# New step costs and a GpSimd wait in the timing model that orders the instructions of a two-layer diffusion block

## The chip, the core and the metric

The kernel runs on one core of a Trainium2 chip. A core has five engines that run side by side, each with its own queue of instructions in program order: TensorE (PE in the profile; PEld is its weight load), VectorE (DVE), ScalarE (ACT), GpSimd (POOL) and SyncE (SP). The time of a run is device microseconds from launch to end. Three timed runs of the kernel before gave 1829.44, 1833.56 and 1835.29 us, median 1833.56 us.

## The reference

Two layers over 512 latent tokens and 256 context tokens, width 1024, all in fp32:

```python
for i in range(DEPTH):                                   # DEPTH = 2
    sh1, sc1, g1, sh2, sc2, g2 = adaln(c, ada_w[i], ada_b[i])
    h_lat = modulate(rms_norm(x, norm_mix[i]), sh1, sc1)
    h_ctx = modulate(rms_norm(ctx, norm_mix[i]), csh1, csc1)
    if i % 2 == 0:   # 8 window-attention heads (a sink each) and 8 neighbourhood heads
        y_lat, y_ctx = even_mixer(h_lat, h_ctx, ...)
    else:            # latent attention: 16 heads, q and k of 64 + 32 columns
        y_lat, y_ctx = odd_mixer(h_lat, h_ctx, ...)
    x = x + g1 * y_lat
    x = x + g2 * squared_relu_mlp(modulate(rms_norm(x, norm_mlp[i]), sh2, sc2), mlp_w1[i], mlp_w2[i])
    # in layer 0 the context tokens get the same two updates
```

In both mixers heads are normalised (and partly rotated), scores are `q @ k` over the token's own selection and all 256 context keys in one softmax, and `p @ v` is projected with the output weights.

## The kernel before

Each fp32 operand of a product is split in a high and a low half (names with `h` and `l`: `wh_`, `wl_`, `hh_`, `hl_`), and a product is three TensorE matmuls. A split is a rounding copy (the high half, on ScalarE or VectorE) and a subtraction (the low half, on VectorE or GpSimd).

The kernel is straight-line code that runs through five stages: norms and conditioning; the even mixer (`mixer0`); the first MLP with the even output projection; the odd mixer (`mixer1`); the odd output projection and the second MLP. In a mixer nine or so streams of work are open at once: projections (`g_...` are their PSUM tiles), preparation of q and k (`qr_`, `ur_`, `ut_`, `qt_`, `kt_`, results in `q_`, `k_`, `kb`), scores of one head pair after another (`c_` the context part, `l_` the local part, reductions to `mx_` and `nm_`, exponentials into `P_`), values (`pp_` are transposes of P, `pt_` or `P` their copies, `o_` the products with v, `rs_`/`rb_` the division), and fillers of other stages (`ada_`, `ps_`). A digit in a name is the job and a last one the half: `c410` is the context score of the odd mixer's fifth pair, second half, first head. The window pairs are `a0` to `a3` with the context's own pairs `ac0` to `ac3`; the neighbourhood pairs are `b...`; the odd mixer's eight pairs are `c0` to `c7`.

What is written out next is decided while the kernel is built, by a model of the engines. Every instruction passes through `Engine`, which emits it and calls `Clock.note`: that adds a cost by engine and shape to the engine's time, after the operands are done and the destination is free (`LAG` is added between engines). All instructions therefore carry the line of that wrapper, L120. Three things read the model:

- `begins` and `weave` (lines 205 to 250): each stream stands at a `yield` with what it needs; the one that could start first on TensorE by the model goes on, and a tie goes to the earlier one in the list.
- `pick`, `pick2`, `square`, `scale_by` (lines 414 to 431, 943 to 952): which of two engines takes a copy, a low half, a square or a scaling is the one that the model has free first.
- `Weights.pump` (line 388): a weight that has landed is split when the model says that its raw data and its buffers are there.

The products of the MLPs and the output projections are in loops without `weave`; there the model moves single copies and splits only.

Of the kernel before, what the change touches and what calls it, by code (L numbers as in the profile page):

```python
# [10 lines left out]
F32 = mybir.dt.float32  # L11
# [16 lines left out]
class Clock:  # L28
# [5 lines left out]
    def __init__(self):  # L34
        self.t = defaultdict(float)
        self._done = defaultdict(lambda: (0.0, None))
        self._used = defaultdict(lambda: (0.0, None))

    @staticmethod
    def keys(a):  # L40
# [26 lines left out]
    def note(self, eng, fn, args, kw):  # L67
        aps = [a for a in list(args) + list(kw.values()) if hasattr(a, "tensor") and hasattr(a, "free_size")]
        outs = aps[:1] + [kw[k] for k in ("accum_out",) if k in kw]
        ins = aps[1:]  # L70
        n = max(a.free_size() for a in aps)
        psum = any(a.space == bass.MemoryType.PSUM for a in aps)
        if eng == "pe":
            if fn == "transpose":
                cost = 0.107
            else:
                f = 4 if aps[1].dtype == F32 else 1
                m = aps[0].partition_size()
                cost = max(aps[2].free_size() * f / 2400 * (0.5 if m <= 64 else 1.0),
                           0.107 * (2 if f == 4 and m > 64 else 1))  # L80
                if m <= 32:
                    cost = 0.109
        elif eng == "act":
            cost = (0.19 if psum else 0.094) + n / 1200 + (0.047 if "accum_out" in kw else 0)
        elif eng == "dve":
            two = len(ins) > 1 and ins[1].free_size() > 1
            cost = 0.07 + n / (960 if two or psum or fn.startswith("reduce") else 1920)
        elif eng == "pool":
            cost = 0.14 + n * 2.11 / 1000
        else:  # L90
            b = 1
            for s in outs[0].shape:
                b *= s
            self.t["dma"] = max([self.t["dma"], self.t["pe"]] + [self.used(a, "dma") for a in outs]) + b * 4 / 350e3
            for a in outs:
                self.set_done(a, self.t["dma"] + 2.0, "dma")
            return
        start = self.t[eng]
        for a in ins:
            start = max(start, self.done(a, eng))  # L100
        for a in outs:
            start = max(start, self.used(a, eng))
        end = start + cost
        self.t[eng] = end
        for a in ins:
            self.set_used(a, end, eng)
        for a in outs:
            self.set_done(a, end, eng)
            self.set_used(a, end, eng)
# [2121 lines left out]
```

## Time and profile before

| | |
|---|---|
| median of the runs | 1833.56 us |
| the profiled execution | 1835.26 us |
| its span | 1833.2 us |
| TensorE busy | 1744.4 us, 95% |
| VectorE busy | 1106.3 us, 60% |
| ScalarE busy | 668.1 us, 36% |
| GpSimd busy | 442.1 us, 24% |
| mean granted TensorE clock | 0.978 |

The profile is of one execution; its span is 2.06 us shorter than its time. TensorE's idle time, the span less 1744.4 us, is 88.8 us. Times in a row are microseconds from the start of the span; a group "x4" is four instructions of one kind in a row, and what stands in brackets behind it is the idle time of its engine just before, with the engine and the operation that ended it. Tile names in these rows have their numbers left out, so place and time tell which pair a row belongs to.

### The profile page before, as it was taken

The page shows a single profiled execution, that of the slowest core. Times are in us where ns is not written, and L with a number is a line of the kernel's source. Part 1 is how long each engine was busy: PE and PEld are TensorE (multiplying, and loading weights), DVE is VectorE, ACT ScalarE, POOL GpSimd, SP SyncE. Part 2 cuts the span into 40 slices and gives each one's busy share as a digit, 9 for nine tenths or more (in the row PEclk, how much of TensorE's full clock was granted, in tenths as well). Part 3 has the DMA queues.
Part 4 walks back from the last instruction along what each step waited for, and adds up shares of the span by engine and source line. Part 5 has one row for each costly group of instructions (what it writes and reads, how often), then busy time and mean ns, then how long its engine had stood idle before and what let it go on. Part 6 is the DMA issues. An engine that isn't in the chain of part 4 may idle for free.

```text
span 1833.2 us, 27762 instructions
## 1 busy us (share of the span) xinstructions
PE 1744.4 (95%) x11288; PEld 1469.0 (80%) x11288; DVE 1106.3 (60%) x1930; ACT 668.1 (36%) x1430; POOL 442.1 (24%) x288
## 2 busy tenths in 40 slices
PE   8889999888999999999999998899999999999999
PEld 6777777676878888888888897677665798989897
DVE  6877576755777666455454747778775652525252
ACT  4445444434233123123122234555554242424241
POOL 3212312122212222222221322302120223232322
PEclk9999999999989999999999999899999999999999
DMA  9234400010533334333431221001000223232332
GB/s 294 81 127 124 124 24 21 24 44 12 173 115 115 127 127 136 121 129 121 138 115 58 70 68 40 25 1 36 23 13 1 69 93 92 93 103 85 101 93 81
DMA packets 56400, 157.43 MB, mean 86 GB/s; under 512 B 8241, under 2 KB 18865, under 8 KB 56145
## 3 DMA queue, kind: packets, MB, share of 16 engines
q1 hardware_dynamic: 53760, 152.34, 26.4%
q0 software_dynamic: 1024, 1.51, 0.4%
q10 hardware_dynamic: 1488, 1.81, 0.3%
q8 instruction: 89, 1.46, 0.3%
q14 instruction: 39, 0.31, 0.1%
HBM read 153.54 MB, written 2.11 MB: 85 GB/s over the span
## 4 chain that ended last, share of the span: by engine, by line
PE 76%; DVE 17%; ACT 4%; issue 2%; DMA 1%; POOL 0%; DVEq 0%; ACTq 0%; SPq 0%; POOLq 0%
PE p L120 48%; PE o_c L120 3%; PE g_kqb L120 3%; PE pp_c L120 2%; PE g_oi L120 2%; PE l_c L120 2%; DVE kb L120 1%; PE o_b L120 1%; PE g_qa L120 1%; DVE k_kqb L120 1%; PE o_a L120 1%; PE g_kv L120 1%; PE warm L120 1%; PE pp_a L120 1%; PE c_c L120 1%
## 5 line engine op out<-in xcount | busy, mean ns | idle before, releaser
L120 PE MATMUL p<-hh_m,wh_w 128*128 128x258 f32 (+2 forms) x1024 | 319.0, 311 | 0.0
L120 PE MATMUL p<-hl_m,wh_w 128*128 128x258 f32 (+2 forms) x1024 | 318.8, 311 | 0.0
L120 PE MATMUL p<-hh_m,wl_w 128*128 128x258 f32 (+2 forms) x1024 | 318.6, 311 | 0.0
L120 PE MATMUL p<-ul,wh_w 128*128 128x512 f32 (+1 forms) x768 | 273.0, 355 | 0.0
L120 PE MATMUL p<-uh,wh_w 128*128 128x512 f32 (+1 forms) x768 | 272.2, 354 | 0.0
L120 PE MATMUL p<-uh,wl_w 128*128 128x512 f32 (+1 forms) x768 | 271.7, 354 | 0.0
L120 ACT ACTIVATE wh_w<-raw_w 128x1024 fp32r<-128x1024 f32 x119 | 124.7, 1051 | 288.2 <-PE p L120 288.2
L120 PEld LDWEIGHTS p<-hh_m,wl_w 128*128 128x128 f32 x1024 | 194.3, 190 | 11.1
L120 PEld LDWEIGHTS p<-hl_m,wh_w 128*128 128x128 f32 x1024 | 194.0, 189 | 11.2
L120 PEld LDWEIGHTS p<-hh_m,wh_w 128*128 128x128 f32 x1024 | 193.9, 189 | 11.1
L120 DVE TENSOR_TENSOR wl_w<-raw_w,wh_w 128x1024 fp32r<-128x1024 f32 x79 | 179.5, 2273 | 31.0 <-ACT wh_w L120 30.7
L120 POOL TENSOR_TENSOR ul<-u,uh 128x768 fp32r<-128x768 f32 (+1 forms) x64 | 100.6, 1572 | 364.3 <-DVE uh L120 364.3
L120 POOL TENSOR_TENSOR wl_w<-raw_w,wh_w 128x1024 fp32r<-128x1024 f32 x49 | 124.0, 2530 | 261.9 <-ACT wh_w L120 210.4
L120 DVE SCALAR_TENSOR_TENSOR x<-p,mod,x 128x512 f32<-128x512 f32 x96 | 60.2, 657 | 203.8 <-PE p L120 203.8
L120 PEld LDWEIGHTS p<-uh,wh_w 128*128 128x128 f32 x768 | 145.2, 189 | 21.2
L120 PEld LDWEIGHTS p<-uh,wl_w 128*128 128x128 f32 x768 | 145.0, 189 | 21.0
L120 PEld LDWEIGHTS p<-ul,wh_w 128*128 128x128 f32 x768 | 145.1, 189 | 20.5
L120 DVE SCALAR_TENSOR_TENSOR dots<-dot_raw,dots 128x1024 f32<-128x1024 f32 x80 | 125.1, 1564 | 39.7 <-DMA dot_raw<-in_ada_t_dram 38.5
L120 ACT ACTIVATE r<-r,bs_p 128x256 f32<-128x256 f32 x64 | 39.5, 617 | 176.1 <-DVE r L120 174.9
L120 DVE TENSOR_TENSOR r<-p,fr_m 128x256 f32<-128x256 f32 (+1 forms) x128 | 60.4, 482 | 53.2 <-PE p L120 51.2
L120 DVE CAST uh<-u 128x768 fp32r<-128x768 f32 (+1 forms) x64 | 31.6, 494 | 96.8 <-ACT u L120 96.8
L120 PEld LDWEIGHTS pp_c<-ident,P 128*128 128x128 f32 x384 | 43.9, 147 | 33.6 <-issue 28.6
(504 smaller groups left out, 3564.8 us busy)
## 6 DMA issues: line engine op xcount, KB each, us to landing
raw_w<-in_mlp_w_dram SPq DMA_DIRECT2D x128, 512.0 KB, 3.6
dot_raw<-in_ada_t_dram SPq DMA_DIRECT2D x56, 512.0 KB, 4.1
ada_raw<-in_ada_w_dram SPq DMA_DIRECT2D x40, 512.0 KB, 4.7
raw_kqb<-in_e_w_in_dram SPq DMA_DIRECT2D x8, 512.0 KB, 3.9
raw_eo<-in_e_w_out_dram SPq DMA_DIRECT2D x8, 512.0 KB, 3.6
raw_oo<-in_o_w_out_dram SPq DMA_DIRECT2D x8, 512.0 KB, 3.8
raw_oi<-in_o_w_in_dram SPq DMA_DIRECT2D x6, 512.0 KB, 3.6
x_in<-in_xT_dram SPq DMA_DIRECT2D x4, 512.0 KB, 5.1
```

What stands on the lines that cost most here:

```text
L120: r = f(*a, **k)
```

## The change

Only the model's costs change; no line of the computation does. In `Clock.note` the cost of a TensorE step becomes 0.013 us plus its columns at 2.4 GHz (half of that for 33 to 64 output partitions, a quarter for 32 and fewer), at least 0.109 us. Where the rounded sizes of its contraction and output partitions, a pair of 128, 64 or 32, differ from those of the step before it, 0.1 us is added, or 0.2 us when the last one had 32 output columns. GpSimd's cost per element goes from 2.11 to 2.17 ns. A VectorE instruction with two sources of which neither, nor the output, is in PSUM starts at the end of a GpSimd instruction that the model has running at its start; the last eight of these are kept in `shared`.

```diff
@@ -35,6 +35,7 @@
         self.t = defaultdict(float)
         self._done = defaultdict(lambda: (0.0, None))
         self._used = defaultdict(lambda: (0.0, None))
+        self.tiling, self.shared = (128, 128), []
 
     @staticmethod
     def keys(a):
@@ -71,22 +72,22 @@
         n = max(a.free_size() for a in aps)
         psum = any(a.space == bass.MemoryType.PSUM for a in aps)
         if eng == "pe":
-            if fn == "transpose":
-                cost = 0.107
-            else:
-                f = 4 if aps[1].dtype == F32 else 1
-                m = aps[0].partition_size()
-                cost = max(aps[2].free_size() * f / 2400 * (0.5 if m <= 64 else 1.0),
-                           0.107 * (2 if f == 4 and m > 64 else 1))
-                if m <= 32:
-                    cost = 0.109
+            f = 4 if fn != "transpose" and aps[1].dtype == F32 else 1
+            m = aps[0].partition_size()
+            cost = 0.013 + aps[2].free_size() * f / 2400 * (1.0 if m > 64 else 0.5 if m > 32 else 0.25)
+            cost = max(cost, 0.109)
+            side = lambda n: 128 if n > 64 else 64 if n > 32 else 32
+            tiling = side(aps[1].partition_size()), side(m)
+            if tiling != self.tiling:
+                cost += 0.2 if self.tiling[1] == 32 else 0.1
+                self.tiling = tiling
         elif eng == "act":
             cost = (0.19 if psum else 0.094) + n / 1200 + (0.047 if "accum_out" in kw else 0)
         elif eng == "dve":
             two = len(ins) > 1 and ins[1].free_size() > 1
             cost = 0.07 + n / (960 if two or psum or fn.startswith("reduce") else 1920)
         elif eng == "pool":
-            cost = 0.14 + n * 2.11 / 1000
+            cost = 0.14 + n * 2.17 / 1000
         else:
             b = 1
             for s in outs[0].shape:
@@ -100,7 +101,13 @@
             start = max(start, self.done(a, eng))
         for a in outs:
             start = max(start, self.used(a, eng))
+        if eng == "dve" and two and not psum:
+            for b, e in self.shared:
+                if b < start < e:
+                    start = e
         end = start + cost
+        if eng == "pool":
+            self.shared = self.shared[-7:] + [(start, end)]
         self.t[eng] = end
         for a in ins:
             self.set_used(a, end, eng)
```

The two programs have the same 306 SyncE instructions and the same matmuls in another order. VectorE has 1852 instructions before and 1845 after, ScalarE 1155 and 1153, GpSimd 293 and 302. In the even mixer 78 of the 256-column products of `g_qa23` stand among the first window pairs, where before it was some 200 products of `g_qa23` and `g_kqb0`; the other products of these follow in one block behind `o_ac1`, and the transposes `ut_qa23` stand directly ahead of the third pair's `c_a200`. In the odd mixer blocks of `g_kv` and `g_uq` that stood inside a chain of `pp_c` and `o_c` stand between two pairs' scores. The wrapper's line is 120 before and 127 after. Three places follow.

VectorE in the even mixer, between the first and the second local reduction of the window pair a1, first head (`mx_a_1604` before, `mx_a_1548` after). Before:

```order
L120 TENSOR_REDUCE mx_a_1604<-l_a_1606 128x1
L120 TENSOR_TENSOR tt_a_1617<-sum_a_1348 128x4
L120 RECIPROCAL rs_a_1619<-tt_a_1617 128x4
L120 TENSOR_TENSOR w_qa_1627<-y_qa_1612 128x24
L120 TENSOR_TENSOR w_qa_1627<-w_qa_1627,v_qa_1578 128x24
L120 TENSOR_SCALAR w_qa_1627<-w_qa_1627 128x24
L120 TENSOR_TENSOR y_qa_1631<-y_qa_1612,w_qa_1627 128x24
L120 TENSOR_TENSOR oT<-oT,y_qa_1631 128x512
L120 TENSOR_TENSOR oT<-oT,rows_sb 128x512
L120 TENSOR_TENSOR oT<-oT,y_qa_1631 128x512
L120 TENSOR_TENSOR oT<-oT,rows_sb 128x512
L120 TENSOR_TENSOR ur_qa_1554<-ur_qa_1554,y_qa_1631 128x512
```

And now:

```order
L127 TENSOR_REDUCE mx_a_1548<-l_a_1550 128x1
L127 TENSOR_TENSOR tt_a_1558<-sum_a_1326 128x4
L127 RECIPROCAL rs_a_1560<-tt_a_1558 128x4
L127 COPY l_a_1578<-rows_sb 128x1
L127 TENSOR_REDUCE mx_a_1548<-l_a_1578 128x1
L127 TENSOR_TENSOR nm_a_1585<-mx_a_1548 128x2
L127 TENSOR_TENSOR oT<-o_a_1504,rb_a_1593 128x256
```

The preparation of the projection `qa23` (twelve instructions before the next `l_a` reduction, from `w_qa` to the last `oT`) has left this place; the second reduction follows the first at once.

ScalarE in the odd mixer at the fifth pair, second half (`P_10242<-pp_c` and `P_10245<-pp_c` are copies of its transposes). Before:

```order
L120 ACTIVATE P_10242,sum_c_12125<-l_c_12220,nm_c_12225 128x512
L120 ACTIVATE kb<-kt_kv_12252,gains_sb 64x256 x2
L120 ACTIVATE wh_oo_12262<-raw_oo_11537 128x1024
L120 ACTIVATE qr_uq_12108<-g_uq_12180 128x384
L120 ACTIVATE sq_uq_12276<-qr_uq_11933 128x768
L120 ACTIVATE P_10242<-pp_c_12293 128x512
L120 ACTIVATE P_10242<-pp_c_12306 128x512
```

And now:

```order
L127 ACTIVATE P_10245,sum_c_12151<-l_c_12262,nm_c_12267 128x512
L127 ACTIVATE kb<-kt_kv_12289,gains_sb 64x256 x2
L127 ACTIVATE P_10245<-pp_c_12327 128x512
L127 ACTIVATE P_10245<-pp_c_12333 128x512
L127 ACTIVATE P_10245<-pp_c_12349 128x512
```

The weight's high half `wh_oo`, the copy `qr_uq` and the square `sq_uq` no longer stand between `kb` and the copies of the transposes.

TensorE in the odd mixer, from the seventh pair's values to the last pair's second half (`c_c710`), with the tiles' numbers. Before:

```order
L120 MATMUL o_c61_12934<-P1_10242,x1_4972 64x256 x2
L120 MATMUL l_c7010_12986<-kb_9696,D1_10243 128x512 x3
L120 MATMUL l_c7011_12991<-kb_9696,D1_10243 128x512 x3
L120 MATMUL o_c61_12934<-P1_10242,x1_4972 64x256 x2
L120 MATMUL o_c61_12934<-ident_84,rs_c61_12984 64x128 x4
L120 MATMUL c_c710_13014<-kb_9696,D1_10243 128x256 x6
```

And now:

```order
L127 MATMUL o_c61_12934<-P1_10245,x1_4972 64x256 x2
L127 MATMUL o_c61_12934<-ident_84,rs_c61_12971 64x128 x4
L127 MATMUL l_c7010_12994<-kb_9696,D1_10246 128x512 x3
L127 MATMUL l_c7011_12999<-kb_9696,D1_10246 128x512 x3
L127 MATMUL c_c710_13014<-kb_9696,D1_10246 128x256 x6
```

The last products of `o_c61` stood between the local scores and the next `c_c`; now nothing stands there.

## Rows read from the trace of the kernel before

**Rows 1.** The page: busy time and its share of the span by engine; the chain's shares.

```profile
PE 1744.4 (95%) x11288; PEld 1469.0 (80%) x11288; DVE 1106.3 (60%) x1930; ACT 668.1 (36%) x1430; POOL 442.1 (24%) x288
...
PE 76%; DVE 17%; ACT 4%; issue 2%; DMA 1%; POOL 0%; DVEq 0%; ACTq 0%; SPq 0%; POOLq 0%
```

**Rows 2.** Stages: length, busy PE, PEld, DVE, ACT, POOL, then clock, DMA share, GB/s.

```profile
0.00:90.00 90.00, 76.42 (x604) 66.16 (x604) 65.79 (x131) 39.92 (x70) 25.62 (x20) 0.92 0.64 191
90.00:480.00 390.00, 355.14 (x2707) 280.12 (x2706) 256.11 (x576) 171.82 (x514) 88.76 (x90) 0.97 0.23 72
480.00:1085.00 605.00, 600.09 (x3443) 528.36 (x3442) 367.49 (x481) 156.49 (x210) 151.45 (x69) 0.99 0.36 112
1085.00:1470.00 385.00, 355.21 (x2260) 269.31 (x2260) 278.33 (x543) 184.70 (x477) 72.43 (x52) 0.96 0.09 27
1470.00:1834.00 364.00, 357.53 (x2282) 325.08 (x2280) 138.58 (x203) 115.15 (x161) 103.80 (x58) 1.00 0.29 92
```

**Rows 3.** Timeline of TensorE, two products in a row: start, duration, line, form.

```profile
99.32 0.28 PE L120 MATMUL g_qa<-wl_qa,hh_a 128*128 128x256 f32 x1
99.44 0.28 PE L120 MATMUL g_qa<-wh_qa,hl_a 128*128 128x256 f32 x1
```

**Rows 4.** Timeline of POOL and DVE at two GpSimd splits, and a cast undisturbed.

```profile
149.33 2.40 POOL L120 TENSOR_TENSOR wl_kqb<-raw_kqb,wh_kqb 128x1024 fp32r<-128x1024 f32 x1 [4.94 <-ACT wh_kqb L120]
149.38 2.36 DVE L120 TENSOR_TENSOR tt_a<-sum_a 128x4 f32<-128x4 f32 x1
...
331.64 2.40 POOL L120 TENSOR_TENSOR wl_kqb<-raw_kqb,wh_kqb 128x1024 fp32r<-128x1024 f32 x1 [15.96 <-ACT wh_kqb L120]
332.88 1.71 DVE L120 CAST wh_kqb<-raw_kqb 128x1024 fp32r<-128x1024 f32 x1 [0.48 <-PE g_kqb L120]
...
1321.23 0.69 DVE L120 CAST wh_oo<-raw_oo 128x1024 fp32r<-128x1024 f32 x1
```

**Rows 5.** Timeline, the even mixer's waits before scores and transposes, and their operands.

```profile
171.79 0.77 PE L120 MATMUL c_a<-kw_kva,q_qa 128*128 128x256 f32 x4 [1.68 <-ACT P_a L120]
...
279.64 0.63 PE L120 MATMUL pp_ac<-ident,P_ac 128*128 128x128 f32 x4 [1.65 <-DVE k_kqb L120]
...
353.04 0.69 ACT L120 ACTIVATE q_kqb<-ut_kqb,qsc 64x512 fp32r<-64x512 f32 x1 [2.05 <-DVE q_kqb L120]
...
353.09 1.19 PE L120 MATMUL c_b<-k_kqb,q_kqb 128*128 128x256 f32 x4 [4.30 <-DVE q_kqb L120]
...
353.76 0.76 DVE L120 SCALAR_TENSOR_TENSOR q_kqb<-ut_kqb,qsc,q_kqb 64x512 fp32r<-64x512 f32 x1 [0.81 <-ACT q_kqb L120]
```

**Rows 6.** Timeline of TensorE, the odd mixer's waits and what stands around them.

```profile
1132.56 2.74 PE L120 MATMUL r_kr<-ident,y_kr 128*32 128x128 f32 x12 [2.22 <-DVE y_kr L120]
...
1182.47 0.98 PE L120 MATMUL c_c<-kb,D 96*128 96x256 f32 x6 [1.50 <-ACT P L120]
...
1187.15 0.65 PE L120 MATMUL o_c<-P,V 128*64 128x256 f32 x4 [1.42 <-ACT P L120]
...
1323.55 1.12 PE L120 MATMUL o_c<-P,V 128*64 128x256 f32 x4 [3.44 <-ACT P L120]
...
1389.87 0.98 PE L120 MATMUL c_c<-kb,D 96*128 96x256 f32 x6 [2.03 <-ACT P L120]
...
1400.63 1.65 PE L120 MATMUL l_c<-kb,D 96*128 96x512 f32 x6
...
1404.76 0.98 PE L120 MATMUL c_c<-kb,D 96*128 96x256 f32 x6 [1.46 <-ACT P L120]
```

**Rows 7.** Stretches of 5 us around four of these waits, columns as in rows 2.

```profile
170.00:175.00 5.00, 3.32 (x22) 1.93 (x19) 2.92 (x6) 3.65 (x12) 0.00 (x0) 0.74 0.04 15
...
1325.00:1330.00 5.00, 5.00 (x24) 2.54 (x22) 4.56 (x12) 2.69 (x9) 0.00 (x0) 0.55 0.66 211
...
1390.00:1395.00 5.00, 5.00 (x24) 3.99 (x24) 2.31 (x4) 1.75 (x5) 0.00 (x0) 0.66 0.01 3
...
1405.00:1410.00 5.00, 5.00 (x35) 3.47 (x35) 2.93 (x5) 2.42 (x7) 1.08 (x1) 1.00 0.00 0
```

## The prediction

> **What bounds the kernel now.** First the page's busy times and the shares of its chain [rows 1]: TensorE is busy for 1744.4 of 1833.2 us and holds 76% of the chain that ends last, VectorE 17%. A change that removes no product can win only part of TensorE's idle 88.8 us, or of what a lowered clock costs. Second the stages [rows 2]. The length less TensorE's busy time is 13.6, 34.9, 4.9, 29.8 and 6.5 us. The two mixers (90 to 480 and 1085 to 1470) thus hold 64.7 of the idle time, with mean clocks of 0.97 and 0.96. They are also the stages that `weave` orders. In the MLP stages the two orders differ by single splits, which have 4.9 and 6.5 us of idle time beside them; I cost these at nothing, and the TensorE products that hide a split there are on the page's first line. Third, TensorE's timeline in both mixers, wait by wait [rows 5, 6]: the reader is to see that nearly all long waits end on the chain score, reduction, exponential, transposed copy, or on the copies of a prepared q or k. Fourth, windows behind such waits [rows 7].
>
> **Is the new cost the better one?** Two 256-column products start 0.12 us apart [rows 3]; the old formula has 256/2400 = 0.107, the new one 0.013 more, 0.120. A projection of 24 such products was 0.3 us too short in the model. The model therefore saw TensorE run ahead of the other engines, and put filler where a dependent step could already have started. VectorE's wait is there too: at 149.38 an operation on four elements per partition takes 2.36 us and ends with the GpSimd subtraction that started 0.05 us before it [rows 4]. A better cost doesn't shorten an instruction, though. It pays only where the new order covers a wait, so the sum goes wait by wait.
>
> [...]
>
> **The change part by part.** All three parts act through one thing, the order, so the terms are places.
>
> Even mixer, window pair a1. In the trace the second half's first score waits 1.68 us at 171.79 [rows 5], behind exponentials that wait for copies of the prepared q; the 5 us window there has a clock of 0.74, so up to 0.26 x 5 = 1.3 us more is lost to it [rows 7]. The preparation of `qa23` leaves this place, so I take both away: -1.7 and -1.3. (Bounds: nothing, if another step is late there, and -3.0.)
>
> Third pair, a2. That preparation now ends directly ahead of its reader: `ut_qa23`, then `c_a200`. Between them stand a copy on ScalarE and a difference on VectorE. The same two steps took 0.69 and 0.76 us at 353 [rows 5], so +1.5. Bounds: 0, if the transposes wait for their own operands while TensorE has the block of `g_kqb0`; 4.3, which is what TensorE waited at 353.09 behind a longer sequence of the same kind.
>
> First neighbourhood pair. Ahead of the transposes `pp_ac30` at 279.64 TensorE waits 1.65 us for `k_kqb` [rows 5]. Of the products that stand between `o_a31` and these transposes, 15 of `g_vb` and six of `g_kqb` with 256 columns leave (21 x 0.12 = 2.5 us [rows 3]), and six of `g_vb` with 512 columns come in (twice the columns, 0.23 by the pitch above, 1.4 us): +1.1. Bounds: 0 and +2.8, with the 1.7 of a clock fall [rows 7].
>
> Later neighbourhood pairs. The wait of 4.30 at 353.09 is behind VectorE, which loses one copy of a high half of about 0.7 us (the 0.69 and 0.76 of the neighbours [rows 5]) to ScalarE, which was idle for 2.05 us: -0.7. Bounds: 0 and -0.7.
>
> Odd mixer, rotary key. `r_kr` waits 2.22 us at 1132.56 [rows 6]. Some 0.7 us more of `g_kv` products (six of 0.12) stand ahead of it: -0.7. Bounds: 0 and -2.2.
>
> Pairs c0 and c1, first score and first values: waits of 1.50 and 1.42 [rows 6]. Blocks of `g_kv` moved out of the value chain to this gap cover one of them and thin out the other to some 1.8, since a copy of `kt_kv` also moves to ScalarE, whose exponentials release both: 1.8 - 2.9 = -1.1. Bounds: -2.9 and +1.
>
> Fifth pair. `o_c41` waits 3.44 us at 1323.55 [rows 6], behind ScalarE, which had a weight's high half, a copy and a square queued ahead of the copies that `o_c41` needs. In the new order these three are gone from there. What is late next is VectorE: it holds the other copies, and `c_c500` now has 0.7 us of TensorE work ahead of it where it had 2.8. I make this about 1.6 for `c_c500` and 1.45 for `o_c41`, together 3.05: -0.4. The clock: behind the 3.44 wait it was 0.55 for a window of 5 us with TensorE busy all through, 0.45 x 5 = 2.25 [rows 7]. After a wait of 2.03 it was 0.66, after one of 1.68 it was 0.74, after one of 1.46 it stayed at 1.00 [rows 6, 7]. A wait of 1.6 lies between the last two, so I take half: -1.1. Bounds: -5.7 and +1.7.
>
> Last pair. Before `c_c710` the trace has a wait of 1.46 at 1404.76, with 1.2 us of `o_c61` ahead of it. Local scores end at 1400.63 + 1.65 = 1402.28, the score starts at 1404.76, so this step needs 2.5 us from them [rows 6]. Now nothing covers it: +1.0, and the clock, which a wait of 2.03 brought to 0.66 for 5 us (0.34 x 5 = 1.7 [rows 7]): +1.7. Bounds: 0 and +2.7.
>
> Other score gaps: of those that change, c1's second half, c2's and c4's stay above 2.5 us; c1's first half falls from 1.77 to 1.44. I take +0.5 for all of them. GpSimd's nine more instructions and VectorE's seven fewer cost nothing where a product stream hides them; without that cover, rival three.
>
> Sum: -3.0 + 1.5 + 1.1 - 0.7 - 0.7 - 1.1 - 1.5 + 2.7 + 0.5 = -1.2 us. Against the profiled execution of 1835.26 us (span 1833.2 and 2.06 around it) that is 1834.1; this execution lies 1.7 above the median of the runs, 1833.56, so I forecast 1832.4, rounded **1832 us**: no change that can be measured. About 0.3%, 5.5 us, is what a measurement here can tell from none.
>
> **Rivals.**
>
> One: the better model places work better than my places show. For it: in the mixers VectorE's clumps (preparation, then reductions) are what the long waits end on [rows 5, 6], and the DVE part of the order shows one such clump dissolved. Against: the wait at 353.09 is a chain without filler in both orders. If the three longest listed waits go (4.30, 3.44 and 1.68), with the 2.25 and 1.3 of their clocks, it is -13.0: about 1821.
>
> Two, slower: the value chains in the odd mixer, `pp` and `o` in turn, are now contiguous. 54 of 95 copies have under 1.2 us from their transposes to the product that reads them, against 9 before, where a score or a projection stood between. [...] If each of the 45 newly thin places waits only 0.2 us, that is +9, and two more clock falls of 1.7 make +12.4: about 1846. [...] For it: both waits on `o_c` [rows 6] are of this kind. Against: ScalarE and VectorE take the copies in turn and ScalarE is busy for only 184.7 of 385 us [rows 2].
>
> Three, the lock: nine more GpSimd instructions (most are 512 or 1024 columns wide) each block a VectorE instruction by the 1.02 us that the cast lost at 332.88 [rows 4], where the model doesn't know it. All on the path: +9.2, about 1842; with 24% of GpSimd's time used already [rows 1] and most of its new work beside products, a third of that, +3, is likelier, and falls inside the forecast.
>
> **How the numbers follow.** Forecast 0.45, with a spread of some 7 us either way from the bounds above (1825 to 1839); rival one 0.27; rival two 0.18; rival three in its full size 0.10. Faster than 1828.1: all of rival one and a quarter of the forecast, 0.38. Slower than 1839.1: rivals two and three, but a sixth of them, and a little of the forecast, 0.27. The rest, 0.35, is the same. The range reaches from below rival one to rival two: 1815 to 1847.
>
> **What would show it.** In the changed profile: the waits at the places of 171.79 and 1323.55 gone or under 1.6 us; a new wait of 1 to 2 us on the third pair's `c_a`; the last `c_c` at 2.5 us; the mixers' idle time between 60 and 68 us together. Rival one is right if that is under 55, rival two if it is over 72 with most of it on `o_c` in the odd mixer, rival three if VectorE's casts and differences have grown beside GpSimd's. I am wrong altogether if the MLP stages move by more than 3 us.

## The result, and the profile after

The changed kernel takes 1861.67 us (median of four runs, 1859.53 to 1864.22), the one before 1833.19 (1829.44 to 1835.29): ratio 1.0158, 95% interval 1.0137 to 1.0179. It is 28 us slower, and 1832 with a range of 1815 to 1847 was forecast. The profiled execution took 1859.53 us, 24.3 more than that of before.

The page's busy times and the shares of its chain:

```profile
span 1857.6 us, 27786 instructions
...
PE 1753.0 (94%) x11288; PEld 1476.3 (79%) x11288; DVE 1088.9 (59%) x1923; ACT 672.0 (36%) x1428; POOL 469.1 (25%) x297
...
PE 67%; DVE 9%; ACT 2%; issue 1%; DMA 1%; POOL 0%; DVEq 0%; ACTq 0%; SPq 0%
```

Against [rows 1] TensorE does the same 11,288 matmuls in 8.6 us more, and stands idle for 104.6 us (1857.6 - 1753.0) instead of 88.8. So two thirds of the profiled execution's loss is waiting. One third is longer busy time for the same matmuls, at a mean granted clock of 0.974 instead of 0.978.

The stages are cut in each kernel at the same events: the last wait for `wl_qa` before the even mixer, the first and the last product of the first MLP, and the first of the second. The columns are those of [rows 2]. After:

```profile
0.00:71.20 71.20, 56.78 (x467) 47.04 (x467) 52.24 (x87) 36.45 (x62) 24.78 (x16) 0.94 0.76 227
71.20:517.90 446.70, 406.34 (x3012) 327.17 (x3013) 294.69 (x653) 182.12 (x528) 110.50 (x105) 0.96 0.24 74
517.90:1065.80 547.90, 542.67 (x3100) 477.43 (x3099) 320.69 (x423) 139.32 (x181) 146.17 (x63) 0.99 0.36 114
1065.80:1489.70 423.90, 384.90 (x2396) 294.86 (x2395) 278.68 (x558) 197.53 (x494) 82.89 (x56) 0.94 0.09 29
1489.70:1857.60 367.90, 362.27 (x2321) 329.81 (x2319) 142.57 (x206) 116.53 (x163) 104.72 (x59) 1.00 0.30 93
```

The two mixers of before, cut in the same way:

```profile
71.00:509.60 438.60, 403.74 (x3012) 324.96 (x3013) 297.44 (x654) 182.72 (x533) 100.10 (x98) 0.97 0.24 75
...
1058.40:1465.30 406.90, 376.73 (x2396) 288.38 (x2395) 283.55 (x562) 193.11 (x491) 78.78 (x55) 0.96 0.10 30
```

The even mixer is 8.1 us longer, the odd one 17.0; the other three together are 0.7 shorter. In the even mixer 5.5 of the 8.1 is idle time (40.4 against 34.9). In the odd mixer 8.8 of the 17.0 is idle time (39.0 against 30.2) and 8.2 is TensorE's busy time for the same 2396 instructions, at a mean clock of 0.94 instead of 0.96.

Most of the odd mixer's loss lies in one stretch, from the third of its 32 context scores (`c_c`) to the fourteenth. First before, then after:

```profile
1167.80:1260.60 92.80, 86.44 (x593) 62.23 (x594) 72.42 (x156) 49.33 (x141) 16.79 (x13) 1.00 0.07 24
...
1177.20:1286.10 108.90, 96.15 (x618) 68.88 (x618) 80.67 (x173) 56.72 (x156) 22.06 (x16) 0.92 0.08 26
```

It is 16.1 us longer. Of these 6.4 are idle time. 25 more products stand in it, an estimated 3 us at the pitch of 0.12 [rows 3]; the rest goes with the clock, 0.92 where it had been 1.00 throughout.

TensorE's timeline after, at the places of the prediction and where new waits are (idle time before the step in brackets):

```profile
188.31 0.64 PE L127 MATMUL ada_ps<-ada_raw,sT 128*32 128x256 f32 x8 [0.97 <-DMA ada_raw<-in_ada_w_dram]
...
199.98 0.69 PE L127 MATMUL ut_qa<-ident,oT 128*128 128x128 f32 x2 [2.49 <-DVE oT L127]
202.06 1.22 PE L127 MATMUL c_a<-kw_kva,q_qa 128*128 128x256 f32 x4 [0.97 <-DVE q_qa L127]
...
286.21 0.63 PE L127 MATMUL pp_ac<-ident,P_ac 128*128 128x128 f32 x4 [2.21 <-DVE k_kqb L127]
...
363.68 1.19 PE L127 MATMUL c_b<-k_kqb,q_kqb 128*128 128x256 f32 x4 [4.30 <-DVE q_kqb L127]
...
1141.31 1.09 PE L127 MATMUL r_kr<-ident,y_kr 128*32 128x128 f32 x5 [1.72 <-DVE y_kr L127]
...
1177.27 0.97 PE L127 MATMUL c_c<-kb,D 96*128 96x256 f32 x6 [1.44 <-ACT P L127]
...
1195.43 0.39 PE L127 MATMUL c_c<-kb,D 96*128 96x256 f32 x1 [2.48 <-ACT P L127]
...
1205.04 1.12 PE L127 MATMUL o_c<-P,V 128*64 128x256 f32 x4 [4.75 <-ACT P L127]
...
1277.00 0.30 PE L127 MATMUL pp_c<-ident,P 128*128 128x128 f32 x1 [3.39 <-DVE kb L127]
...
1341.31 0.97 PE L127 MATMUL c_c<-kb,D 96*128 96x256 f32 x6 [1.38 <-ACT P L127]
...
1345.99 0.65 PE L127 MATMUL o_c<-P,V 128*64 128x256 f32 x4 [1.43 <-ACT P L127]
...
1427.25 0.98 PE L127 MATMUL c_c<-kb,D 96*128 96x256 f32 x6 [2.88 <-ACT P L127]
```

Several waits that were to shrink did: the wait of 1.68 at 171.79 is gone, 2.22 became 1.72, 3.44 became 1.38 and 1.43 [rows 5, 6]. In the odd mixer the largest new ones are 4.75 at 1205.04, which answers to the 1.42 at 1187.15, and 3.39 at 1277.00. In the even mixer one kind of wait is new: TensorE stands six times, 3.4 us together, for the landing of the filler's weight `ada_raw`, as at 188.31; in before it never does. Row 1205.04 names ScalarE's copy of P as what ended the wait. ScalarE's own row says what it waited for:

```profile
1196.60 0.68 ACT L127 ACTIVATE kb<-kt_kv,gains_sb 64x512 fp32r<-64x512 f32 x1
1201.88 1.18 ACT L127 ACTIVATE kb<-kt_kv,gains_sb 64x512 fp32r<-64x512 f32 x2 [4.60 <-DVE kb L127]
...
1204.39 1.09 ACT L127 ACTIVATE P<-pp_c 128x512 f32<-128x512 f32 x2
```

Its next half of `kb` stood still for 4.60 us until VectorE had done the difference of the half before, and the copies of P are queued behind it. So to VectorE:

```profile
1193.35 0.97 DVE L127 TENSOR_TENSOR nm_c<-mx_c 128x2 f32<-128x2 f32 x1
...
1195.35 1.26 DVE L127 TENSOR_TENSOR qr_uq<-qr_uq,rows_sb 128x256 f32<-128x256 f32 x1
...
1197.85 0.42 DVE L127 TENSOR_TENSOR qr_uq<-qr_uq,y_uq 128x256 f32<-128x256 f32 x1
1198.30 1.57 DVE L127 TENSOR_TENSOR qr_uq<-qr_uq,rows_sb 128x256 f32<-128x256 f32 x1
...
1200.77 0.42 DVE L127 TENSOR_TENSOR qr_uq<-tu_uq 128x256 f32<-128x256 f32 x1
1201.11 0.73 DVE L127 SCALAR_TENSOR_TENSOR kb<-kt_kv,gains_sb,kb 64x512 fp32r<-64x512 f32 x1
```

The difference `kb` starts at 1201.11 behind six and a half us of scaling and rotation of `qr_uq`. Two steps of this rotation take 1.26 and 1.57 us, where an undisturbed one of 128 x 256 takes 0.42, as at 1197.85. Just ahead of it the step `nm_c` takes 0.97 us, where the next one takes 0.16. GpSimd was running at the start of each of the three:

```profile
1193.04 1.26 POOL L127 TENSOR_TENSOR wl_kv<-raw_kv,wh_kv 128x512 fp32r<-128x512 f32 x1 [9.66 <-ACT wh_kv L127]
1194.26 2.06 POOL L127 TENSOR_TENSOR qr_uq<-qr_uq,y_uq 128x256 f32<-128x256 f32 x2
1198.07 1.52 POOL L127 TENSOR_TENSOR sq_kv<-kr_kv 128x768 f32<-128x768 f32 x1 [1.75 <-DVE qr_uq L127]
...
1206.84 0.16 DVE L127 TENSOR_TENSOR nm_c<-mx_c 128x2 f32<-128x2 f32 x1
```

In before the `kb` steps came first on VectorE, from 1182.38 on, and the rotation after them. At 1277.00 the order on VectorE is the same, but there the transposes wait for `kb` itself and not for a copy of P; at the same place in before they waited 0.43 us. First before, then after:

```profile
1187.03 0.43 DVE L120 TENSOR_TENSOR qr_uq<-qr_uq,rows_sb 128x256 f32<-128x256 f32 x1
...
1252.21 0.63 PE L120 MATMUL pp_c<-ident,P 128*128 128x128 f32 x4 [0.43 <-DVE kb L120]
...
1274.27 0.42 DVE L127 TENSOR_TENSOR qr_uq<-tu_uq 128x256 f32<-128x256 f32 x1
1274.61 0.73 DVE L127 SCALAR_TENSOR_TENSOR kb<-kt_kv,gains_sb,kb 64x512 fp32r<-64x512 f32 x1
```

The clock of four stretches behind waits and of the fifth pair's (the last but one):

```profile
1178.00:1183.00 5.00, 5.00 (x25) 3.36 (x23) 4.59 (x12) 1.16 (x3) 3.93 (x3) 0.66 0.39 137
...
1195.00:1200.00 5.00, 4.57 (x20) 3.99 (x20) 4.86 (x9) 2.28 (x7) 2.84 (x2) 0.66 0.19 56
...
1205.00:1210.00 5.00, 4.96 (x20) 2.32 (x20) 2.22 (x6) 1.67 (x3) 0.00 (x0) 0.52 0.00 0
...
1345.00:1350.00 5.00, 4.01 (x28) 2.05 (x28) 4.45 (x13) 2.93 (x6) 0.00 (x0) 1.00 0.01 3
...
1428.00:1433.00 5.00, 5.00 (x23) 3.75 (x23) 2.89 (x5) 1.14 (x3) 0.00 (x0) 0.66 0.00 0
```

### The profile page after: what moved, and what is told of

Same layout as the page of the kernel before. It is cut to its first block, busy times and chain, and to the rows that moved or that the text cites. A ratio compares the mean times of both kernels' runs of the same rounds, so it can differ in the third digit from the quotient of the medians.

```text
span 1857.6 us, 27786 instructions
## 1 busy us (share of the span) xinstructions
PE 1753.0 (94%) x11288; PEld 1476.3 (79%) x11288; DVE 1088.9 (59%) x1923; ACT 672.0 (36%) x1428; POOL 469.1 (25%) x297
## 3 DMA queue, kind: packets, MB, share of 16 engines
q8 instruction: 89, 1.46, 0.3%
HBM read 153.54 MB, written 2.11 MB: 84 GB/s over the span
## 4 chain that ended last, share of the span: by engine, by line
PE 67%; DVE 9%; ACT 2%; issue 1%; DMA 1%; POOL 0%; DVEq 0%; ACTq 0%; SPq 0%
PE p L127 48%; PE o_c L127 4%; PE pp_c L127 3%; PE g_oi L127 2%; PE l_c L127 2%; PE g_kv L127 1%; PE c_c L127 1%; DVE kb L127 1%; PE ps_eo L127 1%; PE g_uq L127 1%; PE g_kqb L127 1%; PE ps_oo L127 1%; DVE mx_c L127 1%; DVE hl_m L127 1%; DVE x L127 1%
## 5 line engine op out<-in xcount | busy, mean ns | idle before, releaser
L127 POOL TENSOR_TENSOR wl_w<-raw_w,wh_w 128x1024 fp32r<-128x1024 f32 x50 | 133.6, 2673 | 252.0 <-ACT wh_w L127 205.7
L127 DVE SCALAR_TENSOR_TENSOR dots<-dot_raw,dots 128x1024 f32<-128x1024 f32 x80 | 116.6, 1458 | 41.1 <-DMA dot_raw<-in_ada_t_dram 40.0
```

Of the source, the lines that this page charges most:

```text
L127: r = f(*a, **k)
```

## The experiments

Three theories were put against each other. **Part**: one of the three parts of the change does the harm. **Draw**: any change of a number gives another order, and the order before was a lucky one. **Balance**: it matters how long the model's TensorE steps are against its VectorE steps, and the change lengthened only TensorE's. After a miss it was given a new form, **ratio**: there is a best proportion of the two, and TensorE's steps can be too short against VectorE's as well as too long. Stage lengths below are cut as above, from one profiled execution each.

**1. The parts alone.**

```diff
 # steps: product step only
-            if fn == "transpose":
-                cost = 0.107
...
+            cost = 0.013 + aps[2].free_size() * f / 2400 * (1.0 if m > 64 else 0.5 if m > 32 else 0.25)
+            cost = max(cost, 0.109)
...
 # tiling: old product step, and only
...
+            if tiling != self.tiling:
+                cost += 0.2 if self.tiling[1] == 32 else 0.1
 # wait: old product step, no tiling, and only
+            cost = 0.14 + n * 2.17 / 1000
...
+        if eng == "dve" and two and not psum:
+            for b, e in self.shared:
+                if b < start < e:
+                    start = e
...
```

> Only the measured product step (0.013 us more for each product, at least 0.109) is in the model; tiling, GpSimd's cost and the wait are as before. If one part carries the loss of 28 us and it is the wait for GpSimd, this run is within 6 us of 1833. If it is the product step, about 1860. If any change of the numbers draws another order and the one before was a lucky draw, slower by 8 to 35 us, with the long waits at places of its own.

> Only the 0.1 or 0.2 us at a change of tiling is added to the model. If the loss comes from the wait for GpSimd or the product step, within 6 us of 1833. If it comes from the tiling cost, which makes the chain of transposes and value products look longer in the model, about 1860 and lost in the odd mixer. If any change of the numbers draws another order, slower by 8 to 35 us.

> Only VectorE's wait for GpSimd and 2.17 ns per element are in the model. If the half-modelled lock does the harm, 1850 to 1865, lost in the odd mixer. If not, within 6 us of 1833. If any change of the numbers draws another order, slower by 8 to 35 us.

| kernel | median, us | ratio to before (95%) | even mixer | odd mixer |
|---|---|---|---|---|
| before | 1834.5 | | 438.6 | 406.9 |
| the change | 1861.7 | 1.0158 (1.0137 to 1.0179) | 446.7 | 423.9 |
| steps | 1861.6 | 1.0150 (1.0135 to 1.0165) | 450.0 | 421.6 |
| tiling | 1859.7 | 1.0139 (1.0120 to 1.0158) | 448.6 | 423.0 |
| wait | 1838.3 | 1.0020 (1.0008 to 1.0032) | 430.2 | 417.0 |

The row of before is the median of the 13 runs beside the three variants; the change's ratio is to the 1833.2 us beside its own. Either TensorE cost alone loses what the whole change loses: the losses don't add, so it isn't one part. The wait for GpSimd costs 4 us, with 8.4 won in the even mixer and 10.1 lost in the odd one; the draw theory had said 8 us or more. That pointed to what `steps` and `tiling` have in common: TensorE's steps grow in the model and nothing else does. The longest wait of `steps` in the odd mixer stands where VectorE prepares q (in its numbering the wrapper is L116):

```profile
1162.25 0.63 PE L116 MATMUL qt_uq<-ident,qr_uq 128*96 128x128 f32 x2 [5.61 <-DVE qr_uq L116]
```

**2. Are the losses local?** `m0new` has the new model up to the odd mixer, `m0wait` the wait alone up to there.

```diff
     def mixer1(fold, proj, M):
+        ck.new = False
```

> The whole new model up to the end of the first MLP, the old one from the start of the odd mixer. From the trace of the changed kernel the even mixer lost 7.8 us and the odd one 17.0: if the losses are local to their mixers, 1841 +- 4. If the odd mixer's loss is a consequence of the model's state that the even one hands over (its engines' clocks), 1855 or more.

> Only the wait for GpSimd and 2.17 ns per element, and these only up to the start of the odd mixer; the old model from there. In the run with the wait alone the even mixer was 8.4 us shorter than before and the odd one 10.2 longer. If the mixers' gains and losses are local, 1824 to 1830, faster than before. If the odd mixer's order depends on the state handed over, 1835 or more.

`m0new`: 1843.8 us (ratio 1.0052, 1.0032 to 1.0073), odd mixer 406.7. `m0wait`: 1828.8 us (0.9974, 0.9962 to 0.9987), even mixer 430.0, odd 406.9. Both came out as local losses do. With the old costs the odd mixer gets back its old length, whichever even mixer stands ahead of it.

**3. TensorE's cost the other way, and VectorE's.** In the model VectorE's fixed part is 0.07 us in both kernels. Rows of before, VectorE at the odd mixer's second pair:

```profile
1181.62 0.18 DVE L120 TENSOR_TENSOR w_uq<-y_uq 128x32 f32<-128x32 f32 x1
1181.83 0.19 DVE L120 TENSOR_TENSOR w_uq<-w_uq,v_uq 128x32 f32<-128x32 f32 x1
1182.05 0.18 DVE L120 TENSOR_SCALAR w_uq<-w_uq 128x32 f32<-128x32 f32 x1
...
1182.38 0.73 DVE L120 TENSOR_SCALAR kb<-kt_kv,gains_sb 64x512 fp32r<-64x512 f32 x1
1183.15 0.75 DVE L120 SCALAR_TENSOR_TENSOR kb<-kt_kv,gains_sb,kb 64x512 fp32r<-64x512 f32 x1
```

From start to start a dependent step on 32 elements takes 0.21 us, where the formula gives 0.07 + 32/960 = 0.10, and `kb` 0.77, where it gives 0.07 + 512/960 = 0.60. A fixed part of 0.17 brings these to 0.20 and 0.70.

```diff
 # pe094, pe103: the model before, and
+        if eng == "pe":
+            cost *= 0.94          # 1.03
 # dve17after: the change, and
-            cost = 0.07 + n / (960 if two or psum or fn.startswith("reduce") else 1920)
+            cost = 0.17 + n / (960 if two or psum or fn.startswith("reduce") else 1920)
 # dve12after, dve22after: 0.12, 0.22; dve17before: 0.17 in the model before
```

Only `Clock.note` is changed; `pick` and `pick2`, which have VectorE's cost in formulas of their own, keep 0.07.

> The model before with every TensorE cost times 0.94 (farther from the measured pitch). Theory balance: the too short TensorE steps make up for VectorE steps that the model has too short as well, so that more TensorE work is put ahead of each reader; then a still shorter step costs nothing: 1825 to 1840. Theory draw: each change of a number gives a new order, the one before was a good draw, so 1840 to 1865, whichever way the number moves.

> The model before with every TensorE cost times 1.03, about half of what the measured step adds to a product of 512 columns and a quarter of that for 256. Theory balance: part of the loss of the measured step alone (27 us), so 1838 to 1852. Theory draw: anything from 1835 to 1865, not between the old order and the measured step by rule.

> The changed kernel with 0.17 instead of 0.07 us as the fixed part of every VectorE step in the model (in the trace of before a copy from PSUM of 64 x 512 takes 0.77 us from start to start, the old formula says 0.60; a dependent step on 24 elements 0.21, the formula 0.10). Theory balance: with both engines longer the balance is back, and at least half of the 28 us: 1830 to 1848. Theory draw: 1840 to 1865 like any other draw.

> The changed kernel with 0.12 us as the fixed part of a VectorE step (0.07 gave 1861.7, 0.17 gave 1832.5). Theory balance, in which the size of the step decides and 0.17 is near the trace: between the two, 1838 to 1855. Theory draw: 0.17 was a lucky number, this one 1840 to 1865 or anything else, above 0.22's or below it.

> The changed kernel with 0.22 us as the fixed part of a VectorE step, longer than most rows of the trace show. Theory balance: past the best point, but on the safe side, with more TensorE work ahead of each reader: 1828 to 1845. Theory draw: 1840 to 1865 more likely than not.

> The model before with 0.17 us as the fixed part of a VectorE step and nothing else changed. Theory balance: TensorE's steps now are the short ones against VectorE's, as in the run with 0.94, so 1842 to 1860. If 1825 to 1838, a longer VectorE step helps or is harmless by itself, and it is not the ratio of the two engines that decides but VectorE's steps being too short. Theory draw: 1840 to 1865.

With 0.17 beside the change, the loss is gone: 1832.5 us, ratio 0.9992 (0.9979 to 1.0005), even mixer 435.6, odd mixer 402.0. The odd mixer's longest wait there:

```profile
1395.36 1.01 PE L127 MATMUL c_c<-kb,D 96*128 96x256 f32 x3 [2.88 <-ACT P L127]
```

Of the other five two came out as the balance theory had it, and three did not. 0.94 is slower, 1854.7 us (1.0123, 1.0095 to 1.0151), where it had said harmless: a miss. 1.03: 1842.2 (1.0050, 1.0027 to 1.0073), as it said, but the draw allowed that too. 0.12 won nothing, 1859.9 (1.0139, 1.0123 to 1.0154): a miss. 0.22: 1842.9 (1.0050, 1.0035 to 1.0065), within. 0.17 in the model before is slower, 1841.2 (1.0037, 1.0022 to 1.0052), just under the lower end of what it said. The draw theory's wider figures held in all five; 1832.5 is outside them.

**4. Short VectorE, ratio or draw.** VectorE at 0.17 with each of the three TensorE costs that had lost most.

```diff
 # d17steps, d17tiling, d17pe094: as steps, tiling and pe094, and
-            cost = 0.07 + n / (960 if two or psum or fn.startswith("reduce") else 1920)
+            cost = 0.17 + n / (960 if two or psum or fn.startswith("reduce") else 1920)
```

> Product step alone as in the run that gave 1861.6 (odd mixer 421.6 us), with 0.17 us as the fixed part of a VectorE step. Theory short VectorE: the odd mixer is lost wherever the model has VectorE's queue done too early, whatever TensorE's cost is, so with 0.17 the odd mixer takes 400 to 411 us and the run 1828 to 1846. Theory draw: the odd mixer falls anywhere in 400 to 428, as likely above 413 as below.

> Tiling cost alone as in the run that gave 1859.7 (odd mixer 423.0 us), with 0.17 us for VectorE. Theory short VectorE: odd mixer 400 to 411, run 1828 to 1846. Theory draw: odd mixer anywhere in 400 to 428.

> TensorE times 0.94 as in the run that gave 1854.7 (odd mixer 428.0 us), with 0.17 us for VectorE. Theory short VectorE: odd mixer 400 to 411, run 1828 to 1846. Theory ratio (TensorE against VectorE, which has its best point between): TensorE is short twice over, so odd mixer over 413 and run over 1850. Theory draw: odd mixer anywhere in 400 to 428.

Medians in us by the two costs; the odd mixer's length in brackets:

| TensorE in the model | VectorE 0.07 | VectorE 0.17 | difference |
|---|---|---|---|
| times 0.94 | 1854.7 (428.0) | 1862.6 (427.5) | +7.9 |
| as before | 1834.3 (406.9) | 1841.2 (407.3) | +6.9 |
| product step | 1861.6 (421.6) | 1838.9 (410.5) | -22.7 |
| tiling | 1859.7 (423.0) | 1847.2 (412.2) | -12.5 |
| both, and the wait | 1861.7 (423.9) | 1832.5 (402.0) | -29.2 |

The last three rows go down with a longer VectorE step, the first two up. In the odd mixer, though, the first two don't move (428.0 and 427.5, 406.9 and 407.3). Their loss lies elsewhere: with 0.94 the even mixer is 5.7 us longer and the start 2.6; in the model before the start and what follows the odd mixer are 6.8 longer, the even mixer and the first MLP 4.2 shorter.

That VectorE's short step alone does the harm falls with `d17pe094`: 1862.6 us (ratio 1.0145, 1.0118 to 1.0171), and a wait longer than any of the changed kernel's:

```profile
1155.42 0.63 PE L122 MATMUL qt_uq<-ident,qr_uq 128*96 128x128 f32 x2 [6.75 <-DVE qr_uq L122]
```

The ratio theory had said just this, over 413 us and over 1850. `d17steps` (1.0025, 1.0011 to 1.0039) is within the figures of short VectorE and `d17tiling` (1.0069, 1.0045 to 1.0092) 1 us outside on both; for these two the ratio theory had no figures of its own.

The draw isn't excluded. All three odd mixers lie in its 400 to 428 us. A new draw for one of the slowest kernels would be expected to come out lower, and one for a lucky order higher, which gives four of the five signs of the table; only 0.94 speaks against it. 0.12 should have won something by the balance theory and didn't, and 0.22 lies 10 us above 0.17. What is shown is that a longer TensorE step alone loses 25 to 27 us in either form, and that a longer VectorE step beside it takes back 12 to 29. That the ratio of the two is the reason is likely, and not shown.

**5. The stages that were best, put together.** `best` has the wait for GpSimd with the old costs up to the odd mixer, the change with 0.17 in it, and the old model behind it.

```diff
...
+            cost = (0.17 if self.mode == 1 else 0.07) + n / (960 if two or psum or fn.startswith("reduce") else 1920)
...
+        if self.mode < 2 and eng == "dve" and two and not psum:
...
     def mixer1(fold, proj, M):
+        ck.mode = 1
...
+        ck.mode = 2
         O.give(M)
```

> The wait for GpSimd alone with the old costs up to the odd mixer (430 us in it, as in two runs), the whole new model with 0.17 us for VectorE in the odd mixer (402 us in one run), the old model after it (364 us). If the stages add up, 1834 - 8.5 - 4.8 = 1821, with 1816 to 1827. If the odd mixer draws another order from the state handed over, 1828 to 1845.

It takes 1826.3 us, ratio 0.9958 (0.9944 to 0.9973): 0.4% faster than before, and inside the 1816 to 1827 on record. Its mixers:

```profile
73.30:503.70 430.40, 401.97 (x3011) 326.19 (x3012) 293.96 (x649) 182.45 (x534) 105.13 (x100) 0.96 0.24 76
...
1052.40:1453.80 401.40, 376.34 (x2395) 288.99 (x2394) 269.53 (x539) 203.53 (x508) 82.61 (x56) 0.96 0.09 29
```

Together they are 13.7 us shorter than before's. About 4 us of that is given back behind the odd mixer (372.2 against 367.9), and 2.3 in the start.

## Why the prediction was wrong

The step that failed is the forecast for "Pairs c0 and c1, first score and first values": 1.8 - 2.9 = -1.1. In place of 1.50 and 1.42 stand 2.48 and 4.75, +4.3, and clocks of 0.66 and 0.52 in the windows behind them. I had named the copy of `kt_kv` that moved to ScalarE, and counted it as 0.3 us on the exponentials. I had not followed VectorE's queue, on which the `qr_uq` clump moved ahead of the difference that this copy's successor waits for. The 3.39 at 1277.00 is the same step at another pair, where TensorE had waited 0.43, and stood in no term. These two places alone give 4.3 + 3.0 of the odd mixer's 8.8 us of idle time. All the terms of the odd mixer together came to about nothing; it lost 17.0.

The even mixer's four terms sum to -1.1, and it grew by 8.1. 3.4 us of this stood in no term: those in which TensorE waits for the landing of `ada_raw`. The new order puts this filler ahead of its data; the prediction counts filler as cover, and never as a wait of its own.

Behind both is likely a wrong step in "Is the new cost the better one?". That section held TensorE's new cost against TensorE's rows and took it for the better one; it never held VectorE's cost against VectorE's rows, where steps were too short as well (0.10 for 0.21, 0.60 for 0.77). With both lengthened the loss is gone; with TensorE's cost moved either way alone it is 8 to 27 us. That the proportion of the two is the reason is not shown, as said above.

Point by point:

- Window pair a1, -3.0: right. The wait is gone; the clock, 0.74 before, didn't fall there.
- Third pair, +1.5: the place was right, the size too small. The transposes waited for their own rotated operand too, 2.49 + 0.97 = 3.46 us. That is within the bounds of 0 and 4.3, but the block of `g_kqb0` didn't hide it. The clock fell here too, to 0.67 from 203 to 208, another 1.7 us (an estimate, 0.33 x 5) that no term had.
- First neighbourhood pair, +1.1: 2.21 for 1.65, +0.6.
- Later pairs, -0.7: the wait of 4.30 is unchanged.
- Rotary key, -0.7: 1.72 for 2.22, -0.5.
- Fifth pair, -0.4 and -1.1: 1.38 + 1.43 = 2.81 for 3.44, -0.6, against the 3.05 that I had worked out. The clock stayed at 1.00, so all of the 2.25 went, where half of it was counted.
- Last pair, +1.0 and +1.7: 2.88 for 1.46, +1.4, and 0.66 for 5 us, +1.7.
- MLPs at nothing: right; 548.8 us became 547.9, and 367.9 stayed.
- Rival two had the side and the stage, not the mechanism. The mixers' idle time is 79.4 us (40.4 and 39.0), over the 72 that was its sign, but little of it is on `o_c`: waits of over a microsecond are only the 4.75 and the 1.43 there. All the odd mixer's waits under 0.25 us come to 0.8, where 45 thin places at 0.2 would have made 9. The 0.2 at each place is shown by no run. In the trace of before copies on ScalarE start 0.04 us behind their transposes (the median of 75) and take 0.60, those on VectorE take 0.69, and a product that waits starts 0.05 behind its copy.
- Rival three is not what made the loss: to know the wait cost 4 us by itself (`wait`), and the steps that stood still at 1193 to 1200 are two-source ones, whose wait the model knows. In the trace of the changed kernel the steps of 0.97, 1.26 and 1.57 us all end within 0.3 us behind a GpSimd instruction that was running when they started. What holds a step there no run shows; the lock is my name for it.

The bounds failed too. The upper ends of the terms sum to 13.0 us, and the highest rival, with thin waits and two clock falls, came to +12.4; the profiled execution lost 24.3. No case had a falling clock along a whole row of pairs, though the busy time at the lower clock alone is 8.2 us of the odd mixer's loss.

What stays open: that this queue order makes the harm was not tried by moving that one step. The kept traces speak for it in part. In all seven kernels whose odd mixer takes 417 us or more, VectorE has the clump of `qr_uq` ahead of `kb` at one or two pairs, and starts the difference 4.2 to 8.2 us behind the last transpose of `kt_kv`. So it does in two of the ten kernels below 414 us, `dve17before` and `d17steps`, so one such place is not the whole loss. `steps`, `tiling`, `pe094`, `pe103` and `d17pe094` have another long wait, 5.6 to 6.8 us for `qr_uq` at the first pair, which the changed kernel has not. What the other part of the even mixer's loss hangs on was not followed.

## What to carry to other kernels

In a planner that orders by which engine is free first, a cost that is corrected for one engine alone can make the order worse, as it did here by 25 to 27 us. Correct the costs of all engines together, and time the result: that the proportion matters is likely here, luck of the order isn't excluded. When a planner's numbers change, don't sum the waits at the places that are seen to move; follow each engine's queue between a producer and its reader, above all where a copy changes its engine and the next step stays on another. And where single variants differ by some 10 us by luck of the order, keep the best model for each stage: the mixers' lengths carried over from one build to another within 1 us.

## What the runs showed of the hardware

The clock behind a wait isn't told by that wait's length: behind 1.44 us at 1177.27 it was 0.66 for 5 us, behind 1.38 and 1.43 at 1341 and 1346 it stayed at 1.00. My step from wait to clock, "1.46 leaves it, 1.68 lowers it", was no rule. Such shares are means over 5 us. Behind the wait of 4.75 there is a stretch in which each window of 1 us reads 0.50:

```profile
1204.00:1209.00 5.00, 3.96 (x16) 2.02 (x16) 2.79 (x7) 2.05 (x4) 0.00 (x0) 0.50 0.00 0
```

Four products of `o_c` at 1205.04 took 1.12 us there; at 1.00 the four at 1345.99 took 0.65.

A step on two elements per partition (`nm_c` at 1193.35) took 0.97 us beside a GpSimd step that had started before it, where the next one took 0.16 at 1206.84. It lies on the path from the scores' maximum to the exponentials.
